# The low half of split weights: a subtraction on VectorE against an accumulating DMA on the negated high half

## The chip, the cores and the metric

The kernel runs on one core of one Trainium2 chip. The metric is the device time of one execution in microseconds (us); three executions of the kernel before took 793.93, 794.14 and 794.63 us, so the median is 794.14 us.

## The reference, cut to what matters

The reference is one layer of a diffusion backbone in float32: 512 latent tokens and 256 context tokens of width 1024 go through one combined input projection into two token mixers (latent attention with 4 heads, and a two-directional gated recurrence, HGRN, with 4 heads), an output projection, and a gated feed-forward network of inner width 2816.

```
h = modulate(rmsnorm(x)), hc = modulate(rmsnorm(ctx))
cq, ckv, kpe, hq, hi, hg, ff, fb = split(h @ w_in)          # same for hc
x = x + gt1 * (concat(attention, hgrn) @ w_out)
h2 = modulate(rmsnorm(x))
x = x + gt2 * ((silu(h2 @ w_gate) * (h2 @ w_up)) @ w_down)
out = rmsnorm(x)
```

Every large product is made to near float32 accuracy out of reduced-precision products. A matrix W is split as W = hi + lo, where hi is W rounded to the format float32r and lo = W - hi, and the other operand likewise; the product is then hi·hi + hi·lo + lo·hi.

## The kernel before, in words

**Blocks of weights.** All weights of the large products stand in a list `units` (lines 103 to 115) of 105 blocks, each 128 partitions by up to 1024 columns of float32 (512 KB): blocks 0 to 24 are the input projection (`wi`), 25 to 28 the attention up-projections (`wqkv`; block 26 has 512 columns), 29 to 36 the output projection (`wo`), 37 to 80 gate and up of the feed-forward network in turn (`wgu`), and 81 to 104 its down projection (`wd`), three blocks for each of eight output tiles: two of 1024 columns and one of 768.

**Making a block.** `make_unit(i)` (lines 119 to 134) loads block i into a tile `wf` by a DMA issued from SyncE's queue (SP), lets ScalarE (ACT) round it into `wh` (line 132, named CAST in the trace) and lets VectorE (DVE) subtract `wh` from `wf` into `wl` (line 133). The tiles `wf`, `wh` and `wl` have three buffers each. `wf` is free for another load when line 133 is done with it; `wh` and `wl` are free when the last matmul that reads them is done. Blocks 33 to 36 have buffers of their own (`rh`, `rl`), and so has block 40 (`xh`, `xl`). `unit(i, ahead)` makes all blocks up to i + ahead before block i is used, so block i+2 is asked for just before the matmuls of block i; since three buffers go round, it takes the buffer of block i-1.

**Using a block.** `mm3` (lines 148 to 152) issues three matmuls: high by high (line 150), a product with one low half (151) and a product with the other (152). In most places the weights are the stationary operand, and then `wl` is first read by the third matmul of a block. In the feed-forward network a block of 1024 columns gives 24 matmuls of 512 columns. For the last of the eight output tiles (line 1053) the tokens are done in two halves of 256, which makes the first pass over its blocks half as long.

**The order on the engines.** The kernel is written with a tile framework. It works out one fixed order of instructions for each engine ahead of time, from the order of the program, priorities and its own model of durations, and each engine then runs its list strictly in order; an instruction that waits for a semaphore holds up what stands behind it on the same engine. The list of the GpSimd engine (POOL) holds a few memsets, four additions `a2` in the recurrence (line 592), and a copy with two memsets for the attention's keys (lines 830 to 832); no DMA is issued from it.

**Neighbours that matter.** `late_mod` (lines 422 to 429) loads 32 further blocks (`wl<-in_wmt_dram` in the trace: the load's name, the tile is one of the three `wf` buffers) and reduces each on VectorE. `gates` (line 467) evaluates two sigmoids on ScalarE after each gate projection. `mla_kpe` (line 709), `make_q`, `make_qr`, `make_v` and `make_k` (lines 762 to 803) lead over to the attention, with high and low halves made by a copy on ScalarE and a subtraction on VectorE. `wout`, `add_sq` and `norm2` (lines 931 to 968) are the output projection, the squares for the second norm, and that norm.

Of the kernel before, what the change touches and what calls it, by code (L numbers as in the profile page):

```python
# [10 lines left out]
F32 = mybir.dt.float32  # L11
# [3 lines left out]
AF = mybir.ActivationFunctionType  # L15
ALU = mybir.AluOpType
# [36 lines left out]
def block_kernel(ctx: ExitStack, tc: tile.TileContext, xT, ctxT, vec, cin, cst, msk, wm, wmt, wi, wqkv, wo, wgu, wd, out):  # L53
    nc = tc.nc
# [7 lines left out]
    def nm(s):  # L62
        uid[0] += 1
        return f"{s}_{uid[0]}"
# [47 lines left out]
    for n in range(KT):  # L112
        for part in range(3):
            w = UNIT if part < 2 else DFF - 2 * UNIT
# [4 lines left out]
    def make_unit(i):  # L119
        kind, src, w = units[i]  # L120
        f = L0.tile([P, UNIT], F32, tag="wf", name=nm("wf"), bufs=3)
        nc.sync.dma_start(f[:, :w], src)
        if kind == "wo" and i >= WO0 + 4:
            hi = stage["pool"].tile([P, UNIT], F32R, tag="rh", name=nm("rh"), bufs=4)
            lo = stage["pool"].tile([P, UNIT], F32R, tag="rl", name=nm("rl"), bufs=4)
        elif i == GU0 + 3:
            hi = N2.tile([P, UNIT], F32R, tag="xh", name=nm("xh"), bufs=1)
            lo = N2.tile([P, UNIT], F32R, tag="xl", name=nm("xl"), bufs=1)
        else:
            hi = L0.tile([P, UNIT], F32R, tag="wh", name=nm("wh"), bufs=3)  # L130
            lo = L0.tile([P, UNIT], F32R, tag="wl", name=nm("wl"), bufs=3)
        nc.scalar.copy(hi[:, :w], f[:, :w])  # L132
        nc.vector.tensor_sub(lo[:, :w], f[:, :w], hi[:, :w].bitcast(F32))  # L133
        made.append((hi, lo))

    WO0 = NW_IN + 4
# [3 lines left out]
    def prefetch(n):  # L140
        while len(made) < min(n, len(units)):
            make_unit(len(made))
# [1020 lines left out]
```

## Time and profile before

One execution was profiled. It took 792.62 us, of which 790.8 us are its span, from the first instruction to the last.

| engine | busy us | share of the span |
|---|---|---|
| TensorE, matmuls (PE) | 768.1 | 97% |
| VectorE (DVE) | 446.9 | 57% |
| ScalarE (ACT) | 311.4 | 39% |
| GpSimd (POOL) | 10.1 | 1% |
| DMA, queue of SyncE | 87.03 MB | 33.0% of 16 engines |

The mean granted clock of TensorE was 0.988. A line such as "L133 DVE TENSOR_TENSOR wl<-wf,wh x100 | 119.6, 1196 | ..." is read thus: line 133 of the kernel ran 100 times on VectorE, writing `wl` from `wf` and `wh`, was busy for 119.6 us in all and 1196 ns each; behind the second bar stands the time for which the engine had been idle just before, and what ended that. Buffer numbers are left out of the names. Matmuls overlap in the pipeline, so that one shown with 0.39 us follows the one before it after 0.23 us.

### The profile page before, as it was taken

What the parts mean: (1) busy time and instruction counts of PE and PEld (TensorE: products, weight loads), DVE (VectorE), ACT (ScalarE), POOL (GpSimd) and SP (SyncE); (2) the same over time, 40 slices, a digit from 0 to 9 for tenths busy, and PEclk for the clock granted to TensorE, in tenths of its full rate; (3) what the DMA queues carried; (4) which work ended last, traced back from release to release, by engine and by line L of the source; (5) the groups of instructions that cost most, each with busy time, mean ns of one, the idle gap of its engine ahead of it and who ended that gap; (6) DMA issues with size and microseconds to landing.
All of it is one profiled execution on the core that took longest, in us unless ns stands there. A gap on an engine that the chain in (4) does not pass through costs nothing.

```text
span 790.8 us, 10832 instructions
## 1 busy us (share of the span) xinstructions
PE 768.1 (97%) x4342; PEld 631.7 (80%) x4342; DVE 446.9 (57%) x820; ACT 311.4 (39%) x569; POOL 10.1 (1%) x18
## 2 busy tenths in 40 slices
PE   8899999999999989999999999999999999999995
PEld 7568878788887768888999888888888888888885
DVE  5576569839778989985566434432333233223324
ACT  6344246434544577664344223222322222212211
POOL 0000000000000100000000000000000000000000
PEclk8899999999999999999999999999999999999997
DMA  9923723311110022345403343423232323332303
GB/s 332 390 76 134 252 80 108 133 57 55 64 55 28 28 80 90 125 165 181 160 2 100 113 160 133 151 89 107 80 107 82 104 78 96 93 100 80 111 3 107
DMA packets 26706, 88.77 MB, mean 112 GB/s; under 512 B 2976, under 2 KB 5280, under 8 KB 26528
## 3 DMA queue, kind: packets, MB, share of 16 engines
q1 hardware_dynamic: 25568, 87.03, 33.0%
q10 hardware_dynamic: 1088, 1.05, 0.4%
q8 instruction: 34, 0.56, 0.3%
q14 instruction: 16, 0.13, 0.1%
HBM read 85.97 MB, written 2.10 MB: 111 GB/s over the span
## 4 chain that ended last, share of the span: by engine, by line
PE 89%; DVE 7%; ACT 2%; issue 1%; DMA 1%; SPq 0%; DVEq 0%; ACTq 0%
PE big L150 18%; PE big L151 17%; PE big L152 17%; PE sm L150 9%; PE sm L151 9%; PE sm L152 9%; PE big L857 2%; PE sm L604 1%; PE sm L876 1%; PE big L858 1%; PE sm L320 1%; DVE U L585 1%; PE sm L598 1%; DVE acl L309 1%; DVE G L506 1%
## 5 line engine op out<-in xcount | busy, mean ns | idle before, releaser
L133 DVE TENSOR_TENSOR wl<-wf,wh 128x1024 fp32r<-128x1024 f32 (+2 forms) x100 | 119.6, 1196 | 186.3 <-ACT wh L132 186.2
L132 ACT CAST wh<-wf 128x1024 fp32r<-128x1024 f32 (+2 forms) x100 | 102.9, 1029 | 280.3 <-PE big L151 167.6
L150 PE MATMUL big<-h2h,wh 128*128 128x512 f32 (+1 forms) x368 | 140.3, 381 | 0.0
L151 PE MATMUL big<-h2l,wh 128*128 128x512 f32 (+1 forms) x368 | 140.0, 381 | 0.0
L152 PE MATMUL big<-h2h,wl 128*128 128x512 f32 (+1 forms) x368 | 140.0, 381 | 0.0
L151 PEld LDWEIGHTS big<-h2l,wh 128*128 128x128 f32 x368 | 69.2, 188 | 14.6
L150 PEld LDWEIGHTS big<-h2h,wh 128*128 128x128 f32 x368 | 69.2, 188 | 14.4
L152 PEld LDWEIGHTS big<-h2h,wl 128*128 128x128 f32 x368 | 69.2, 188 | 14.4
L150 PE MATMUL sm<-ah,wh 128*128 128x512 f32 (+1 forms) x198 | 73.5, 371 | 0.0
L152 PE MATMUL sm<-ah,wl 128*128 128x512 f32 (+1 forms) x198 | 73.4, 371 | 0.0
L151 PE MATMUL sm<-al,wh 128*128 128x512 f32 (+1 forms) x198 | 73.4, 370 | 0.0
L427 DVE SCALAR_TENSOR_TENSOR wl<-wl,cs 128x1024 f32<-128x1024 f32 x32 | 39.0, 1220 | 33.8 <-DMA wl<-in_wmt_dram 33.8
L150 PE MATMUL big<-wh,hh 128*128 128x512 f32 x96 | 40.2, 422 | 3.3 <-ACT hh L340 1.9
L150 PEld LDWEIGHTS sm<-ah,wh 128*128 128x128 f32 x198 | 37.3, 188 | 7.1
L151 PEld LDWEIGHTS sm<-al,wh 128*128 128x128 f32 x198 | 37.3, 188 | 7.1
L152 PEld LDWEIGHTS sm<-ah,wl 128*128 128x128 f32 x198 | 37.3, 188 | 7.1
L150 PE MATMUL big<-hh,wh 128*128 128x512 f32 x104 | 42.8, 412 | 0.0
L151 PE MATMUL big<-hl,wh 128*128 128x512 f32 x104 | 40.9, 394 | 0.0
L152 PE MATMUL big<-hh,wl 128*128 128x512 f32 x104 | 40.8, 392 | 0.0
L151 PE MATMUL big<-wl,hh 128*128 128x512 f32 x96 | 38.8, 406 | 0.0
L152 PE MATMUL big<-wh,hl 128*128 128x512 f32 x96 | 38.4, 402 | 0.0
L506 DVE RECIPROCAL G<-S 128x528 f32<-128x528 f32 x8 | 27.5, 3432 | 0.1
(326 smaller groups left out, 1353.4 us busy)
## 6 DMA issues: line engine op xcount, KB each, us to landing
wf<-in_wgu_dram SPq DMA_DIRECT2D x44, 512.0 KB, 3.4
wl<-in_wmt_dram SPq DMA_DIRECT2D x32, 512.0 KB, 3.5
wf<-in_wi_dram SPq DMA_DIRECT2D x25, 512.0 KB, 3.9
wf<-in_wd_dram SPq DMA_DIRECT2D x16, 512.0 KB, 3.5
wms<-in_wm_dram SPq DMA_DIRECT2D x11, 512.0 KB, 9.6
wf<-in_wo_dram SPq DMA_DIRECT2D x8, 512.0 KB, 3.5
wf<-in_wd_dram SPq DMA_DIRECT2D x8, 384.0 KB, 3.1
wm<-in_wm_dram SPq DMA_DIRECT2D x5, 512.0 KB, 10.2
```

What stands on the lines that cost most here:

```text
L132: nc.scalar.copy(hi[:, :w], f[:, :w])
L133: nc.vector.tensor_sub(lo[:, :w], f[:, :w], hi[:, :w].bitcast(F32))
L150: nc.tensor.matmul(o, lh, rh, start=start, stop=False, skip_group_check=True)
L151: nc.tensor.matmul(o, lh, rl, start=False, stop=False, skip_group_check=True)
L152: nc.tensor.matmul(o, ll, rh, start=False, stop=stop, skip_group_check=True)
L309: nc.vector.tensor_add(acc_, acc_, sq_)
L320: nc.tensor.matmul(ps[32 * g : 32 * g + 32, :256], csil[:, 4 * j + kk, :], f[:, kk * 256 : (kk + 1) * 256], start=(j == 0), stop=(j == 1), ...
L427: nc.vector.scalar_tensor_tensor(f, f, 1.0, sc, op0=ALU.mult, op1=ALU.mult, accum_out=acc)
L506: nc.vector.reciprocal(I, S)
L585: nc.vector.scalar_tensor_tensor(U[:, c1, :], U[:, c0, :], er[:, 1, c0 : c0 + 1], U[:, c1, :], op0=ALU.mult, op1=ALU.add)
L598: nc.tensor.matmul(t, a2[:, j, :], vt[:, j, h * P : (h + 1) * P], start=True, stop=False, skip_group_check=True)
L857: nc.tensor.matmul(ps[:, 0, :], L, R[:, :NL], start=(i == 0), stop=(i == 4), skip_group_check=True)
```

## The change

Blocks 0 to 7 are made as before. From block 8 on, ScalarE writes the negated rounded weight into the low tile (a copy with scale -1), a DMA issued from GpSimd's queue adds the float32 block onto it in SBUF (the destination is viewed as float32, so lo = f - round(f)), and ScalarE rounds the block into the high tile in a second pass. VectorE has no part in these 97 blocks. `wf` is now free when both that DMA and the second pass have read it, and the first matmul that reads the low half waits for the DMA.

```
-        nc.scalar.copy(hi[:, :w], f[:, :w])
-        nc.vector.tensor_sub(lo[:, :w], f[:, :w], hi[:, :w].bitcast(F32))
+        if i < 8:
+            nc.scalar.copy(hi[:, :w], f[:, :w])
+            nc.vector.tensor_sub(lo[:, :w], f[:, :w], hi[:, :w].bitcast(F32))
+        else:
+            nc.scalar.activation(lo[:, :w], f[:, :w], AF.Copy, scale=-1.0)
+            nc.gpsimd.dma_start(lo[:, :w].bitcast(F32), f[:, :w], accum_op=ALU.add)
+            nc.scalar.copy(hi[:, :w], f[:, :w])
```

## The prediction

> **What bounds the kernel now.** I read the page first: who is busy, the chain that ended last, and the two groups that the change touches.
>
> ```profile
> span 790.8 us, 10832 instructions
> ...
> PE 768.1 (97%) x4342; PEld 631.7 (80%) x4342; DVE 446.9 (57%) x820; ACT 311.4 (39%) x569; POOL 10.1 (1%) x18
> ...
> PE 89%; DVE 7%; ACT 2%; issue 1%; DMA 1%; SPq 0%; DVEq 0%; ACTq 0%
> ...
> L133 DVE TENSOR_TENSOR wl<-wf,wh 128x1024 fp32r<-128x1024 f32 (+2 forms) x100 | 119.6, 1196 | 186.3 <-ACT wh L132 186.2
> L132 ACT CAST wh<-wf 128x1024 fp32r<-128x1024 f32 (+2 forms) x100 | 102.9, 1029 | 280.3 <-PE big L151 167.6
> ```
>
> TensorE is busy for 768.1 of 790.8 us and holds 89% of the chain. The subtraction takes VectorE 1196 ns and the rounding takes ScalarE 1029 ns, each 100 times (five more blocks with buffers of their own stand in other groups). Neither is a bound on average, so I look at where TensorE has gaps, by stage (columns: window, its length, then busy time and count for PE, PEld, DVE, ACT, POOL, then clock, DMA share, GB/s).
>
> ```profile
> 230.00:300.00 70.00, 65.38 (x493) 50.89 (x493) 60.21 (x123) 44.60 (x104) 5.05 (x5) 1.00 0.15 49
> 300.00:366.00 66.00, 64.17 (x370) 54.97 (x369) 55.31 (x109) 41.33 (x83) 0.00 (x0) 1.00 0.42 144
> 366.00:420.00 54.00, 54.00 (x394) 51.04 (x393) 36.25 (x76) 24.67 (x46) 0.00 (x0) 1.00 0.27 88
> 420.00:640.00 220.00, 220.00 (x988) 179.29 (x987) 85.39 (x100) 66.51 (x83) 0.00 (x0) 1.00 0.34 113
> 640.00:762.00 122.00, 122.00 (x523) 98.11 (x522) 36.22 (x43) 29.27 (x39) 0.00 (x0) 1.00 0.29 87
> ```
>
> From 366 to 762 us TensorE has no gap: nothing can be won there, only lost, if a low half comes late. The gaps that a lighter VectorE could close lie in 230 to 300 us, the last recurrence head and the passage into attention: 70.00 − 65.38 = 4.62 us. Two of the waits there are on VectorE:
>
> ```profile
> PE big L150 <- DVE krl L720: 1.6, 1, 1.6
> ...
> PE sm L604 <- DVE U L585: 0.6, 1, 0.6
> ```
>
> **What the change moves.** VectorE loses 97 subtractions, 97 × 1.196 = 116 us. ScalarE gains 97 passes; I price one like the rounding of the same shape, 97 × 1.029 = 100 us. GpSimd gains 97 DMA issues, the DMA engines 97 transfers that read two blocks and write one. SP issues what it issued, but a `wf` buffer now comes free only when the transfer has landed.
>
> **How late is the low half?** No row shows an accumulating DMA or a DMA issued from GpSimd. The nearest rows are plain loads and GpSimd's own arithmetic:
>
> ```profile
> wf<-in_wgu_dram SPq DMA_DIRECT2D x44, 512.0 KB, 3.4
> ...
> wf<-in_wd_dram SPq DMA_DIRECT2D x8, 384.0 KB, 3.1
> ...
> x<-in_xT_dram SPq DMA_DIRECT2D x1, 2048.0 KB, 7.8
> ```
>
> ```profile
> 267.18 1.27 POOL L592 TENSOR_TENSOR a<-am,am 128x512 f32<-128x512 f32 x1 [27.58 <-DVE am L559]
> ```
>
> A plain load of 512 KB lands after 3.4 us, four times as much after 7.8 us, so each further 512 KB costs (7.8 − 3.4)/3 = 1.5 us. An accumulation reads twice: 3.4 + 1.5 = 4.9 us. For the issue I take one GpSimd instruction, 1.27 us: L = 6.2 us from the end of the negation to the landing. The lower end is a plain load, 3.4 us; the upper is three in a row (both reads one after the other, behind a weight load in flight), 10.2 us. I take 6.2 because the engines are mostly free (DMA share 0.29 to 0.34 in the feed-forward stages). For 384 KB I take 0.7 us less, 5.5 us.
>
> [...]
>
> **Where L is covered.** In the gate and up stage one block's rounding starts when its buffer is released, and this is its first low use:
>
> ```profile
> 559.12 1.05 ACT L132 CAST wh<-wf 128x1024 fp32r<-128x1024 f32 x1 [2.04 <-PE big L151]
> ...
> 570.78 0.40 PE L152 MATMUL big<-h2h,wl 128*128 128x512 f32 x1
> ```
>
> That is two blocks of matmuls and a little, 11.66 us. The negation has to wait for the last L152 rather than the last L151 (one matmul, 0.2 us later) and takes 1.05 us: L may be 11.66 − 0.2 − 1.05 = 10.4 us. In the down projection two blocks can be 24 + 18 instead of 48 matmuls, 11.2 × 42/48 = 9.8 us, and L may be 9.0 us. With 6.2 both stages cost nothing, and the cover is two blocks of matmuls; beyond 9.0 us the excess would appear in every round of three blocks.
>
> **Term 1, the last head (+1.05 us).** The rounding of a later block stands ahead of the sigmoids, released by the same projection:
>
> ```profile
> 231.76 1.05 ACT L132 CAST wh<-wf 128x1024 fp32r<-128x1024 f32 x1 [3.45 <-PE big L151]
> ...
> 232.71 0.81 ACT L470 ACTIVATE sg<-big 128x768 f32<-128x768 f32 x1
> ...
> 236.09 1.26 DVE L496 TENSOR_TENSOR_SCAN S<-G,reset 128x528 f32<-128x528 f32 x1 [0.51 <-ACT G L493]
> ```
>
> Now two passes stand there. The sigmoids, and behind them the scan for which VectorE sits idle already, come 1.05 us later; that chain ends in the 0.6 us wait of L604, so the whole pass shows. Bounds 0 (the order puts a pass elsewhere) to 1.05.
>
> **Term 2, ACT before attention (+0.9 us).** ScalarE alone, in order:
>
> ```profile
> 282.94 1.04 ACT L132 CAST wh<-wf 128x1024 fp32r<-128x1024 f32 x1
> 285.41 0.28 ACT L610 ACTIVATE osq<-sm 128x128 f32<-128x128 f32 x1 [1.42 <-PE sm L604]
> ...
> 296.06 0.85 ACT L768 CAST knh<-sm 128x512 fp32r<-128x512 f32 x2
> ```
>
> From 285.41 on it runs with almost no gap to the keys at 296.06, for which the first scores wait. Two blocks are made in the 5 us before: 2 × 1.05 = 2.1 us extra, against 1.42 us of idle here; with the negation's later start I put 0.9 us on this run. One VectorE subtraction in the same stretch (1.2 us) goes, which helps only if ScalarE is not late: bounds −1.2 to +1.0.
>
> **Term 3, the krl wait (−0.9 us).**
>
> ```profile
> 269.26 1.21 DVE L133 TENSOR_TENSOR wl<-wf,wh 128x1024 fp32r<-128x1024 f32 x1
> 270.49 0.42 DVE L720 TENSOR_TENSOR krl<-big,krh 64x256 fp32r<-64x256 f32 x1
> ```
>
> This subtraction stands right ahead of the `krl` step that frees TensorE's bank (the 1.6 us wait). Without it the step could start about 1.2 us earlier, but ScalarE's copies from that bank come next; I take 0.9 of it. Bounds −1.2 to 0.
>
> **Term 4, the tail (+0.7 us).** The last output tile is done in halves, so its blocks are needed sooner:
>
> ```profile
> 758.34 1.05 ACT L132 CAST wh<-wf 128x1024 fp32r<-128x1024 f32 x1 [4.57 <-PE sm L151]
> ...
> 762.51 0.84 ACT L132 CAST wh<-wf 128x768 fp32r<-128x768 f32 x1 [3.12 <-PE sm L151]
> ...
> 765.60 0.28 PE L152 MATMUL sm<-ah,wl 128*128 128x256 f32 x1
> ...
> 768.41 0.28 PE L152 MATMUL sm<-ah,wl 128*128 128x256 f32 x1
> ```
>
> Each negation starts about 0.2 us after the cast did (the last L152). Block 103 is negated by 758.5 + 1.05 = 759.55 and lands at 765.75 against a need at 765.60. Block 104: 762.75 + 0.84 + 5.5 = 769.1 against 768.41, 0.7 us late, and this is TensorE's last work: it adds to the end in full. Bounds 0 (L up to 4.8) to 4.5 (L = 10.2).
>
> **Term 5, output projection (+1.0 us).** Here casts wait for loads, and the squares of the norm stand behind them on ScalarE:
>
> ```profile
> 382.61 1.05 ACT L132 CAST xh<-wf 128x1024 fp32r<-128x1024 f32 x1 [2.72 <-DMA wf<-in_wgu_dram]
> ...
> 394.45 0.42 ACT L938 ACTIVATE sqt<-x 128x256 f32<-128x256 f32 x1 [2.40 <-DVE x L951]
> ...
> 397.48 0.26 ACT L190 ACTIVATE rsr<-sm,epst 128x2 f32<-128x2 f32 x1 [1.31 <-PE sm L174]
> ```
>
> Each of the three `wf` buffers is held about 5 us longer (1.05 + 6.2 against 1.03 + 1.2); blocks 38 to 40 are two reuses behind block 32, so their casts move from about 383 to 393 us. If ScalarE's order stays, the last square slips about 3.5 us past 394.87 and TensorE, in order, stands at the sums; if the order adapts, nothing. Bounds 0 to 3.5; I take 1.0, nearer to the adapted order, since the framework orders by its own durations.
>
> GpSimd's other work (four additions, one copy, two memsets) waits behind transfers whose negation waits for TensorE; I cost it at nothing, since TensorE uses those results only several us later. If that cover is gone, the additions delay L598 by up to one issue, 1.3 us.
>
> Sum: 1.05 + 0.9 − 0.9 + 0.7 + 1.0 = +2.75 us: 792.62 + 2.75 = 795.4 us for a profiled execution; the median of the runs lies 1.5 us above the profiled one (794.14), so 796.9 us. A measurement of this kernel can tell about 0.2%, 1.6 us, from no change.
>
> **Rivals.** *Hidden everywhere (0.28):* terms 1, 2 and 5 fall into idle time, leaving the tail less part of term 3: about +0.5 us, 794.6. For it: ScalarE is 39% busy, and 100 us more make 52%. Against it: the two places where ScalarE has no room.
>
> *VectorE was the bound between 230 and 300 us (0.12):* ScalarE's passes fall into its gaps (the 1.42 us), and the removed subtractions come off the chain: −0.9, −1.2 and the 0.6 us of L604: −2.7 us, 791.4. For it: VectorE is busy 60.21 of 70 us there. It decides if the second pass does not precede the sigmoids.
>
> *The low half lands late (0.15):* at L = 10.2 the down projection loses 1.2 us in each of seven rounds, 8 us, the tail 4.5, the output projection 3.5: with terms 1 to 3 about +17 us, 811. It decides from L = 9.0 on. For it: no row shows such a transfer, and GpSimd may be slow to issue. Against it: DMA share near 0.3. [...]
>
> **How the numbers follow.** The forecast has 0.45 (own range 795.8 to 800), the rivals as above. Slower by over 0.2%: 0.45 + 0.15 = 0.60; within: 0.28; faster: 0.12. The range 793 to 806 takes in the hidden case and the start of the late one; it leaves out most of the faster rival and the far half of the late one.
>
> **What would show it.** Right: GpSimd's DMAs landing 5 to 8 us after the negation; no gap on TensorE between 420 and 760 us; a gap near 768 us of up to 1 us before an L152; the scan near 236 us about 1 us later; the krl wait under 1 us. Wrong: waits of TensorE on `wl` in the feed-forward stages (late landing), or a shorter 230 to 300 us stage (VectorE was the bound). A different order of ScalarE around 380 to 400 us settles term 5.

## The result, and the profile after

The changed kernel took 822.68 us (median of 818.55, 819.25, 826.12 and 826.85) against 794.05 us for the kernel before on the same chip: a ratio of 1.036 [1.029, 1.043]. On a second chip it was 820.27 against 792.99 us, 1.036 [1.031, 1.040]. So it is slower, as forecast, but by 28.6 and 27.3 us instead of 2.75, far beyond the range of 793 to 806.

The page of the changed kernel (826.12 us, span 824.2):

```profile
span 824.2 us, 11070 instructions
...
PE 782.5 (95%) x4342; PEld 640.9 (78%) x4342; DVE 339.6 (41%) x723; ACT 396.8 (48%) x666; POOL 94.4 (11%) x115
...
q0 software_dynamic: 13968, 49.55, 33.0%
q1 hardware_dynamic: 25568, 87.03, 31.9%
...
PE 63%; DMA 18%; DVE 8%; ACT 5%; issue 5%; SPq 1%; POOL 0%; DVEq 0%; ACTq 0%; POOLq 0%
...
L138 ACT CAST wh<-wf 128x1024 fp32r<-128x1024 f32 (+2 forms) x92 | 94.3, 1025 | 232.4 <-PE big L156 84.8
...
L137 POOL DMA_DIRECT2D wl<-wf x92 | 79.4, 863 | 544.9 <-ACT wl L136 466.8
...
L136 ACT ACTIVATE wl<-wf 128x1024 fp32r<-128x1024 f32 (+2 forms) x92 | 94.9, 1032 | 26.0 <-DMA wf<-in_wi_dram 15.1
...
wl<-wf POOLq DMA_DIRECT2D x83, 512.0 KB, 5.7
wf<-in_wgu_dram SPq DMA_DIRECT2D x44, 512.0 KB, 4.8
```

VectorE is 107 us lighter and ScalarE 85 us heavier (116 and 100 were worked out). What the forecast did not have stands in two other rows: DMA holds 18% of the chain (1% before), and the new queue q0 takes 33.0% of the sixteen DMA engines, as much as all loads together (q1). By the time of its packets that is 0.330 × 824.2 / 97 = 2.8 us of all sixteen for one accumulation; a load of 512 KB (0.524 MB) takes 0.319 × 824.2 × 0.524 / 87.03 = 1.6 us. A `wgu` load now lands after 4.8 us, before after 3.4.

The windows of time that the prediction showed for the kernel before, with the same columns (the work in them stands 7 to 33 us later, so they do not hold quite the same stages):

```profile
230.00:300.00 70.00, 64.43 (x519) 50.76 (x519) 54.94 (x126) 41.99 (x101) 10.86 (x11) 0.99 0.36 82
300.00:366.00 66.00, 60.94 (x327) 52.07 (x326) 50.42 (x98) 45.29 (x83) 1.72 (x2) 0.90 0.39 114
366.00:420.00 54.00, 49.17 (x276) 42.22 (x275) 17.41 (x36) 27.00 (x42) 7.06 (x9) 0.97 0.80 207
420.00:640.00 220.00, 214.16 (x1044) 178.18 (x1045) 52.90 (x106) 99.33 (x132) 29.52 (x35) 0.98 0.75 185
640.00:762.00 122.00, 122.00 (x523) 98.16 (x523) 12.18 (x20) 50.77 (x64) 19.35 (x23) 1.00 0.84 186
```

TensorE, without a gap from 366 to 762 us before, now has gaps up to 555 us and none after; the DMA share has gone from about 0.3 to 0.75 to 0.84; and the clock (the third column from the end) is below 1.00 in four of five rows. What TensorE waits for (us in total, times, longest):

```profile
PE sm L179 <- DVE sqa L945: 4.5, 1, 4.5
PE big L157 <- DMA wl<-wf: 2.9, 4, 1.3
PE big L862 <- ACT pp L868: 2.8, 1, 2.8
PE big L155 <- DVE qnl L781: 2.7, 1, 2.7
...
PE sm L157 <- DMA wl<-wf: 2.3, 1, 2.3
PE sm L881 <- DVE oml L892: 2.2, 1, 2.2
```

Only two rows are waits on the low half itself, 5.2 us in all. The longest is the wait for the squares of the norm, term 5. Its cause can be read in two views of the same stretch, first ScalarE's list in order of time (in brackets its idle time and what ended it):

```profile
398.11 1.06 ACT L136 ACTIVATE rl<-wf 128x1024 fp32r<-128x1024 f32 x1 [7.14 <-DMA wf<-in_wo_dram]
...
410.46 1.06 ACT L136 ACTIVATE wl<-wf 128x1024 fp32r<-128x1024 f32 x1 [5.95 <-DMA wf<-in_wgu_dram]
411.42 0.71 ACT L943 ACTIVATE sqt<-x 128x256 f32<-128x256 f32 x2
...
414.20 1.06 ACT L136 ACTIVATE wl<-wf 128x1024 fp32r<-128x1024 f32 x1 [1.13 <-DMA wf<-in_wgu_dram]
...
418.48 1.06 ACT L136 ACTIVATE xl<-wf 128x1024 fp32r<-128x1024 f32 x1 [1.96 <-DMA wf<-in_wgu_dram]
```

and the chain of waits:

```profile
385.31 4.57 DMA rl<-wf
389.87 0.02 SPq L122
389.89 0.04 issue
389.94 8.15 DMA wf<-in_wo_dram
...
399.46 4.54 DMA rl<-wf
404.00 0.02 SPq L122
404.02 0.04 issue
404.06 6.29 DMA wf<-in_wgu_dram
```

An accumulation lands at 389.87, and only then is its `wf` free and SP starts the next load, which takes 8.15 us beside the other transfers; once round, 404.00 and 6.29 us. ScalarE stands 5.95 us in front of the negation for that block (block 38), and the squares, which need none of it, stand behind it; 1.13 and 1.96 us more follow in front of the negations for blocks 39 and 40. TensorE is idle from 418.20 to 422.66. I call this a **late load at the head of a line**.

To locate the loss I take, block by block, how much later TensorE first uses it than in the trace before. Its growth by stretch, in us:

| kernel (one profile each) | to block 23 | to 29 | to 33 | to 41 | to 61 | to the end | sum |
|---|---|---|---|---|---|---|---|
| changed | 4.1 | 10.7 | 4.2 | 7.8 | 4.0 | 0.2 | 31.1 |
| changed, second chip (816.12 us) | 1.3 | 7.3 | 3.7 | 7.7 | 1.1 | 0.2 | 21.4 |

Block 2 starts the count: in the first 46 us, before any changed block is used, profiles differ by up to 7 us by chance (most stand 2 to 3 us later than that of before, three 1 us earlier or so, one 5.5 us later), and that is left out here. Blocks 23, 29, 33, 41 and 61 are first used at 234, 355, 382, 430 and 542 us of the trace before.

**The clock.** In the row of 300 to 366 us above the clock column reads 0.90: TensorE is busy for 60.94 us there, part of them at half speed. The trace's clock records give full speed in the kernel before from 24 to 782 us; in the changed kernel they have six stretches of 3.41 or 6.83 us at half clock, behind the gaps of 2.2 to 4.5 us at 148, 295, 310, 340, 395 and 418 us, 27.3 us in all. Half of that, up to 13.7 us, is lost without any wait that a view shows. On the second chip it was 13.7 us at half clock.

### The profile page after: what moved, and what is told of

It reads as the page before. It is cut to its first block, busy times and chain, and to the rows that moved or that the text cites. A ratio compares the mean times of both kernels' runs of the same rounds, so it can differ in the third digit from the quotient of the medians.

```text
span 824.2 us, 11070 instructions
## 1 busy us (share of the span) xinstructions
PE 782.5 (95%) x4342; PEld 640.9 (78%) x4342; DVE 339.6 (41%) x723; ACT 396.8 (48%) x666; POOL 94.4 (11%) x115
## 3 DMA queue, kind: packets, MB, share of 16 engines
q1 hardware_dynamic: 25568, 87.03, 31.9%
q10 hardware_dynamic: 1088, 1.05, 0.4%
## 4 chain that ended last, share of the span: by engine, by line
PE 63%; DMA 18%; DVE 8%; ACT 5%; issue 5%; SPq 1%; POOL 0%; DVEq 0%; ACTq 0%; POOLq 0%
PE big L155 12%; PE big L156 12%; PE big L157 12%; PE sm L155 6%; PE sm L156 6%; PE sm L157 6%; DMA wf<-in_wgu_dram 4%; DMA wl<-wf 4%; DMA wf<-in_wi_dram 4%; DMA wl<-in_wmt_dram 2%; DMA wf<-in_wo_dram 2%; PE big L862 1%; DVE wl L432 1%; PE sm L609 1%; DMA rl<-wf 1%
## 5 line engine op out<-in xcount | busy, mean ns | idle before, releaser
L138 ACT CAST wh<-wf 128x1024 fp32r<-128x1024 f32 (+2 forms) x92 | 94.3, 1025 | 232.4 <-PE big L156 84.8
L137 POOL DMA_DIRECT2D wl<-wf x92 | 79.4, 863 | 544.9 <-ACT wl L136 466.8
L136 ACT ACTIVATE wl<-wf 128x1024 fp32r<-128x1024 f32 (+2 forms) x92 | 94.9, 1032 | 26.0 <-DMA wf<-in_wi_dram 15.1
L1006 DVE TENSOR_TENSOR sgl<-sgl,big 128x512 f32<-128x512 f32 x22 | 15.1, 687 | 161.3 <-ACT sgl L1005 161.3
L155 PEld LDWEIGHTS big<-h2h,wh 128*128 128x128 f32 x368 | 69.2, 188 | 14.1
L1037 DVE SCALAR_TENSOR_TENSOR x<-sm,mod,x 128x512 f32<-128x512 f32 (+1 forms) x9 | 6.2, 691 | 97.6 <-PE sm L157 97.6
```

The source lines that it names most:

```text
L136: nc.scalar.activation(lo[:, :w], f[:, :w], AF.Copy, scale=-1.0)
L137: nc.gpsimd.dma_start(lo[:, :w].bitcast(F32), f[:, :w], accum_op=ALU.add)
L155: nc.tensor.matmul(o, lh, rh, start=start, stop=False, skip_group_check=True)
L1006: nc.vector.tensor_mul(sg, sg, ps[:, 1, :])
L1037: nc.vector.scalar_tensor_tensor(x1[:, n, a : a + w], ps[:, :w], mod[:, 3, n : n + 1], x1[:, n, a : a + w], op0=ALU.mult, op1=ALU.add)
```

## The experiments

Each is compared with the kernel before on its own chip (median, ratio and 95% interval); stretches are those of the table above, in us. First the changed kernel once more:

> The changed kernel once more, on the chip of these runs: 818 to 828 us, with the same places of loss (150, 260 to 300, 311, 340, 395, 418 and 500 to 555 us) if they belong to the kernel; places that are missing here are chance.

Five of those places came again; the gap near 150 us was 1.2 instead of 2.3 us with no half clock behind it, and 500 to 555 us lost 1.1 us instead of 4.0. So those two vary from run to run, which fits the spread of 816 to 827 us.

The theory that I began with: `wf` is held until the accumulation has landed, so loads come late, and a late load at the head of a line does the rest. Rival A: ScalarE's second pass. Rival B: the traffic of the transfers.

**A VectorE addition in place of the transfer** (label e1_dve_add)

```
-            nc.gpsimd.dma_start(lo[:, :w].bitcast(F32), f[:, :w], accum_op=ALU.add)
+            nc.vector.tensor_add(lo[:, :w], f[:, :w], lo[:, :w].bitcast(F32))
```

> The negation and the rounding stay on ScalarE, but the sum that makes the low half is a VectorE addition on the tile instead of a transfer; it computes the same. Theory (the transfer holds a wf buffer for about 6 us, the next load starts that much later, and ScalarE's negation, waiting for that load, blocks what stands behind it): the buffer comes free about 1.2 us after the passes, as before the change, so nearly all of the 28 us goes: 793 to 798 us, no gap of TensorE of 2 us or more after 30 us, no half clock there. Rival A (ScalarE's second pass is what costs): 810 us or more, with the gaps at 148, 296, 311, 340 and 419 us still there.

798.56 against 794.62 us, 1.0052 [1.0030, 1.0074]. Stretches: 0.7, 4.4, 0, 0, 0, 0. Rival A falls for everything from block 29 on; its stages are full again:

```profile
366.00:420.00 54.00, 54.00 (x365) 49.71 (x364) 31.99 (x65) 30.64 (x50) 0.00 (x0) 1.00 0.31 109
420.00:640.00 220.00, 220.00 (x1019) 180.69 (x1018) 86.37 (x109) 101.85 (x124) 0.00 (x0) 1.00 0.32 110
```

But the second pass is not free: 4.4 us between blocks 23 and 29, more than I expected of it (the median lies just above the range of 793 to 798), and there a gap of 3.58 us with half clock behind it.

**The accumulation reads the block from HBM again** (label e2_hbm_cast), so that `wf` is free after ScalarE's passes

```
-            nc.gpsimd.dma_start(lo[:, :w].bitcast(F32), f[:, :w], accum_op=ALU.add)
+            nc.gpsimd.dma_start(lo[:, :w], src, accum_op=ALU.add)
```

> The accumulating transfer reads the weight block from HBM a second time instead of from its wf buffer, so the buffer is free when ScalarE's two passes are done; transfers and their landing stay, and the low half is as late as before or later; it computes the same up to the type in which the sum is rounded. Theory (held buffer, late load): loads start early again, most of the loss goes: 796 to 804 us, and at most the places stay where TensorE waits for wl itself (block 32, blocks 47 to 59: up to 8 us). Rival B (the late landing itself, or the traffic of the transfers, costs): 815 us or more.

816.64 us, 1.026 [1.021, 1.032]. My expectation failed. Stretches: 0, 10.0, 6.5, 0, 1.7, 1.9. Between blocks 33 and 41, where the squares stood behind late loads, the loss is gone (0 instead of 7.8 and 7.7); the other stretches tell less, since before block 23 and behind block 41 the two profiles of the changed kernel differ by about 3 us themselves. But these transfers, which read HBM and write the float32r tile, take longer (median 7.6 us to landing, 5.7 in the changed kernel), and at block 32 TensorE waits 4.8 us for the low half itself:

```profile
383.26 11.49 DMA wl<-in_wo_dram
394.76 0.04 issue
394.80 0.79 PE sm L157
```

So this form has a cost that isn't the held buffer: transfers that take longer, 11.49 us at block 32. How much of it the changed kernel's own transfers have, this run can't tell.

**The negation on GpSimd** (label e5_pool_neg)

```
-            nc.scalar.activation(lo[:, :w], f[:, :w], AF.Copy, scale=-1.0)
+            nc.gpsimd.tensor_scalar(lo[:, :w], f[:, :w], -1.0, None, op0=ALU.mult)
```

> The negation moves from ScalarE to GpSimd; the accumulating transfer stays; ScalarE has a single pass for each block again; it computes the same. Theory (held buffer): the buffer is held as long or longer (GpSimd's pass is no faster than ScalarE's), loads stay late; ScalarE's rounding waits for them in the negation's place: 812 to 830 us. Rival A (ScalarE's second pass costs): 794 to 802 us.

835.99 us, 1.054 [1.051, 1.057]. Rival A falls again: ScalarE has its single pass (311.4 us busy, as before) and the loss is larger. The negation takes 2.7 us on GpSimd (1.03 on ScalarE in the changed kernel), so the low half and the release of `wf` are that much later.

**Only from block 61 on** (label e3_from61)

```
-        if i < 8:
+        if i < 61:
```

> The changed form only from block 61 on (the end of the modulation loads), so 44 of the 97 blocks; it computes the same. Theory: there every block has slack for the landing and no other user of the wf buffers; no loss before 530 us, nothing behind it: 793 to 797 us. Rival B (the transfers' traffic or the low half's landing costs for every block alike): 44/97 of 28 us, 804 to 810 us.

794.19 us, 0.9997 [0.9975, 1.0019]. Stretches: 0 everywhere, 0.1 at the end. 44 of 97 transfers cost nothing, although the DMA engines are as busy as in the changed kernel:

```profile
550.00:640.00 90.00, 90.00 (x388) 72.50 (x387) 11.04 (x16) 40.47 (x49) 13.76 (x16) 1.00 0.83 184
```

**Traffic without a hold, and with one** (labels e7_traffic and e8_hold): the kernel before, and beside it an accumulation into a buffer in HBM that nobody reads

```
+        if i >= 8:   # e7_traffic: hi[:, :w].bitcast(F32) as source; e8_hold: f[:, :w]
+            nc.gpsimd.dma_start(scr[i][:, :w], SOURCE, accum_op=ALU.add)
```

> The kernel before (rounding on ScalarE, subtraction on VectorE), and beside it GpSimd issues for every block from the ninth on an accumulating transfer of the rounded block (wh) into memory that nobody reads: the traffic of the change, but it holds no wf buffer and nobody waits for it; it computes the same. Rival B (traffic): loads take longer and the loss comes back, 805 us or more. Theory (held wf buffer): wh is held some us longer than a matmul needs it at most; 794 to 799 us.

> The same with the transfer reading the wf buffer instead of wh, so that the next load into that buffer waits for the end of the transfer, about 5 us later than before; no second pass on ScalarE, no low half that comes late; it computes the same. Theory (held wf buffer): loss at the places where loads were late after the change (near 150 us, 410 to 440 us, blocks 47 to 59), 8 to 20 us: 803 to 815 us, the difference to the run with wh as source is 8 us or more. Rival B: no more than 3 us apart from the run with wh as source.

812.88 us, 1.022 [1.018, 1.027], and 808.12 us, 1.017 [1.013, 1.021]. For the first my theory said 794 to 799: it fell as the only cause. The second lies in the range that I had set, but it was to be 8 us or more above the first and is 4.8 us below it: neither branch of that expectation came true. Stretches with `wh` as source: 1.4, 3.3, 0, 8.8, 6.6, 0.1; with `wf`: 7.1, 0.6, 0, 2.5, 0, 0. Traffic makes loads late with no `wf` held (`wh` is, but no engine's wait in this trace ended with such a transfer). It is not quite the traffic of the change: it goes to HBM, and its queue takes 36.0% of the engines, 3.0 us for each transfer instead of 2.8:

```profile
scr_dram<-wh POOLq DMA_DIRECT2D x83, 512.0 KB, 5.6
wf<-in_wgu_dram SPq DMA_DIRECT2D x44, 512.0 KB, 5.4
```

and the consequence is the picture of the changed kernel, the squares (L940 here) behind a rounding that waits for its load, after a load of 9.56 us in the chain:

```profile
401.04 1.04 ACT L132 CAST xh<-wf 128x1024 fp32r<-128x1024 f32 x1 [5.96 <-DMA wf<-in_wgu_dram]
401.99 1.04 ACT L132 CAST wh<-wf 128x1024 fp32r<-128x1024 f32 x1
402.93 0.72 ACT L940 ACTIVATE sqt<-x 128x256 f32<-128x256 f32 x2
```

With `wf` as source a load cannot start while the transfer that reads its buffer runs, and from block 29 on less is lost than with `wh`. So hold and traffic do not simply add up.

**Short and long stalls of TensorE** (labels g1_short and g2_long), to price the clock: the kernel before, with a chain of VectorE copies before each of the output tiles 1 to 7 of the down projection

```
+        if n and a == 0:
+            c = N2.tile([P, 256], F32, tag="sqt", name=nm("gap"), bufs=4)
+            nc.vector.tensor_copy(c[:, :W], x1[:, n - 1, :W])
+            for _ in range(K):              # g1_short: W = 32, K = 0; g2_long: W = 256, K = 8
+                nc.vector.tensor_copy(c[:, :W], c[:, :W])
+            nc.vector.tensor_copy(ps[:, :W], c[:, :W])
```

> The kernel before, with seven short stalls of TensorE in the down projection: at the start of output tiles 1 to 7 its accumulator waits for two small VectorE copies behind the step before; it computes the same. About 1.1 us each by the durations of such copies: 7 x 1.1 = 8 us, so 800 to 804 us. Theory of the clock (a gap from about 2 us on is followed by 3.4 us or twice that at half clock, a shorter one is not): no half clock behind them, the loss is the sum of the gaps. Rival: every gap costs clock, 805 us or more.

> The same with chains of ten VectorE copies, seven gaps of about 3 to 4 us; it computes the same. Theory of the clock: behind each gap 3.4 to 6.8 us at half clock, which costs 1.7 to 3.4 us besides: the loss is 1.4 to 2 times the sum of the gaps, 825 to 845 us. Rival (the half clock seen in the trace after has another cause): the loss is the sum of the gaps alone, 815 to 822 us, no half clock.

822.85 us, 1.035 [1.031, 1.040], and 850.68 us, 1.071 [1.067, 1.076]. The "short" stalls were not short: seven of 18.6 / 7 = 2.66 us (the wait row), and a window before, in and behind one of them reads:

```profile
PE sm L150 <- DVE sm L1032: 18.6, 7, 2.8
```

```profile
685.00:692.00 7.00, 7.00 (x31) 5.42 (x29) 1.23 (x1) 1.10 (x2) 0.00 (x0) 1.00 0.35 97
692.00:695.00 3.00, 0.21 (x2) 0.10 (x1) 2.57 (x6) 1.50 (x3) 0.00 (x0) 1.00 0.36 133
695.00:702.00 7.00, 7.00 (x24) 5.58 (x25) 0.00 (x0) 0.00 (x0) 0.00 (x0) 0.76 0.15 52
```

Behind the gap 7 us hold 24 matmuls instead of 31, at 0.76 of the clock. Six of the seven gaps are followed by 3.41 us at half clock. The kernel loses 29.4 us at the end of this trace, of which 18.6 are waits; the other 10.8 are close to half of 6 × 3.41 = 20.5. In the long case the gaps were 5.1 to 5.8 us instead of 3 to 4; all seven (39.3 us of waits) are followed by 6.83 us at half clock, and 57.4 us are lost. So these gaps cost 1.6 and 1.5 times their length on average, and the half clock belongs to gaps, not to this change. A fixed length from which on a gap costs clock, as the expectation had it, does not hold: one of the gaps of 2.79 us here and one of 2.84 us on the second chip (at 307 us) had no half clock behind them, and one of 1.84 us there (at 388 us) had.

**Blocks 29 to 60 alone** (label x1_29to60) **and every second block** (label x2_every2nd)

```
-        if i < 8:
+        if i < 29 or i > 60:     # x1_29to60;  x2_every2nd: if i < 8 or i % 2:
```

> The changed form for blocks 29 to 60 alone (output projection, and the gate and up blocks beside which modulation rows are loaded), 32 of the 97 blocks; it computes the same. Theory (loads, accumulations and modulation loads together come near the capacity of the DMA engines there; with the held buffers that makes loads late): about what the trace after lost between the uses of blocks 29 and 60, some 12 to 16 us: 806 to 812 us. Rival (those losses only follow from the delays before them, or each of the 97 blocks costs alike): 32/97 of 28 us or less, 803 us or less.

> The changed form for every second block only, from the ninth on; it computes the same. Theory (the DMA engines' capacity decides from block 29 on): with half the transfers their share falls to about 0.7 in the gate and up stage, no loss at blocks 41 to 60, at most 4 us in the output projection, half or less of the rest before: 797 to 805 us. Rival (each changed block costs alike): half of 28 us, 808 us.

814.14 us, 1.028 [1.025, 1.030], 2 us above the expected range; stretches -0.2, 5.0, 3.7, 8.2, 2.0, 0.1. And 804.66 us, 1.014 [1.012, 1.017]; 0, 3.0, 0.5, 5.8, 0, 0. A third of the blocks makes 21 of the 27 us that the whole change costs on this chip. One reading is the rate of the DMA engines: in part of the output projection TensorE takes 2.8 us for a block (blocks 33 to 36), while a load and an accumulation take 1.6 + 2.8 = 4.4 us of all DMA engines, and their share is 0.98, 0.97 and 0.93 in the three windows of 10 us from 390 us of the changed kernel. Between blocks 41 and 55 it is 4.4 plus half a modulation load, 5.2 of the 5.6 us that TensorE takes for a block, and behind them 4.4 of 5.6 (estimates from these prices; the measured share is 0.88 from 460 to 555 us, and 0.83 from 560 to 640). With half the transfers that stage is at 0.65 and loses nothing:

```profile
460.00:550.00 90.00, 90.00 (x387) 72.53 (x386) 27.07 (x37) 33.81 (x41) 6.88 (x8) 1.00 0.65 181
```

In the output projection (to 33 and to 41) 6.3 us are left of the 11.9 that blocks 29 to 60 alone lose there. The losses go by stage, not by the number of transfers.

**Blocks 24 to 31 subtracted by GpSimd** (label x5_pool_sub), the version that was to win

```
-        nc.vector.tensor_sub(lo[:, :w], f[:, :w], hi[:, :w].bitcast(F32))
+        eng = nc.gpsimd if 24 <= i < 32 else nc.vector
+        eng.tensor_sub(lo[:, :w], f[:, :w], hi[:, :w].bitcast(F32))
```

> A version meant to win: the kernel before, with the subtraction for blocks 24 to 31 on GpSimd instead of VectorE; no second pass on ScalarE, no transfer; it computes the same. If VectorE's subtraction was what stood ahead of the krl step and the scan between 230 and 300 us, TensorE gains up to 2.7 us: 791 to 794 us against 794. If GpSimd's slower pass makes the low half late for TensorE or holds the wf buffer too long: 795 to 800 us.

809.61 us, 1.021 [1.018, 1.024]: both branches of the expectation were wrong. All 16.2 us are lost between blocks 23 and 29. One part shows: a VectorE step that took 0.68 us before (line 788 there) takes 2.40 us beside a GpSimd pass, and ends 0.55 us after it (VectorE's and GpSimd's lists):

```profile
291.48 2.40 DVE L789 SCALAR_TENSOR_TENSOR m<-m,cs 128x512 f32<-128x512 f32 x1
```

```profile
290.98 2.35 POOL L134 TENSOR_TENSOR wl<-wf,wh 128x1024 fp32r<-128x1024 f32 x1 [4.37 <-ACT wh L132]
```

That stretch has no version here that beats the kernel before.

**Blocks 8 to 23, blocks 24 to 28, and these with an addition** (labels y1_8to23, y2_24to28, y3_24to28_add): the condition set to those blocks, in the last with the VectorE addition shown above

> The changed form for blocks 8 to 23 alone; it computes the same, and TensorE's work stays in the order of the kernel before. Theory (a held wf buffer makes a modulation load or weight load late near 130 to 155 us): 1.5 to 5 us, 795 to 799 us. If the loss near 150 us was chance: 793 to 795 us.

> The changed form for blocks 24 to 28 alone; it computes the same, but TensorE's work near 240 to 300 us stands in the other order that the changed kernel has too. The trace after lost about 5 us between the uses of blocks 23 and 28: 797 to 801 us if these blocks cause it; 793 to 795 us if it followed from earlier delays.

> Blocks 24 to 28 alone with negation and rounding on ScalarE and a VectorE addition, no transfer; it computes the same. If ScalarE's second pass and the order are the cause: as much as with the transfer, within 2 us. If the transfer is the cause: 793 to 795 us.

796.08 us, 1.0030 [1.0007, 1.0053]; 801.29 us, 1.010 [1.005, 1.016]; 798.97 us, 1.0066 [1.0040, 1.0092]. Sums in their profiles: 3.1, 7.1 and 4.4 us. With 18.9 for blocks 29 to 60 and 0.1 from 61 on the parts give 3.1 + 7.1 + 18.9 + 0.1 = 29.2 us, between the two profiles of the whole change and near its 28 us. Of the 7.1 us of blocks 24 to 28, 4.4 come without any transfer, from the second pass and from the other order in which the framework then puts the work (block 24 is begun about 3 us earlier in both runs; block 27 0.4 us later with the addition and 5.6 with the transfer). The other 2.7 us come with the transfer. By the medians the two runs differ by 2.3 us, so neither branch of the last expectation is quite met. How much is the pass and how much the order isn't separated.

**A hold without a transfer** (labels y5_hold_only, two passes; y6_hold_half, one)

```
+        if 29 <= i <= 60:
+            for _ in range(2):
+                nc.gpsimd.tensor_scalar(f[:, :w], f[:, :w], 1.0, None, op0=ALU.mult)
```

> The kernel before, and behind the subtraction of blocks 29 to 60 two GpSimd passes over wf in place (times one), which hold the buffer about 5.4 us longer by the 2.7 us of such a pass; no transfer, no second pass on ScalarE; it computes the same. Theory of the held buffer: most of the 20 us that blocks 29 to 60 lose, 804 to 814 us. Theory of the full DMA engines: 793 to 798 us.

> As the run with two GpSimd passes over wf, with one: blocks 29 to 60 hold their buffer about 2.9 us longer than before, GpSimd is at most half busy in the feed-forward stage; no transfer; it computes the same. Theory of the held buffer: some of the loss is back, in the output projection above all, where a block takes TensorE 2.8 us and three buffers turn round: 797 to 805 us, none in the feed-forward stage. If only GpSimd's own rate made the loss with two passes: 793 to 796 us.

830.55 us, 1.046 [1.042, 1.050], and 797.01 us, 1.0029 [1.0010, 1.0048]. Stretches with two passes: 0, 8.6, 0, 19.0, 7.7, 0.1; with one: -0.2, 2.1, 0, 2.4, 0, 0.1. Loads take 3.4 and 3.2 us (before 3.4), so a hold without any transfer can lose as much and more. But the first of these two runs overshoots, because GpSimd itself was full and held the buffers longer than the 5.8 us of two passes:

```profile
L136 POOL TENSOR_SCALAR wf<-wf 128x1024 f32<-128x1024 f32 x64 | 183.8, 2882 | 124.9 <-DVE rl L133 50.3 <-DVE wl L133 33.0 <-ACT qs L796 21.6
```

```profile
380.00:425.00 45.00, 32.59 (x186) 29.40 (x184) 19.87 (x26) 11.91 (x20) 44.51 (x16) 0.86 0.24 82
```

VectorE is a little slower beside these passes too (its twelve sums of squares between 280 and 440 us took 561 ns each, 422 before), so even this is not a hold and nothing else. A hold of 2.8 us costs 4.4 us where the change loses 18.9, and the change holds about 4.8 us longer than before (1.05 + 6 against 1.03 + 1.2). **What stays open:** which share of the 19 us from block 29 to 60 is the hold and which the full DMA engines. Each costs time without the other (18.7 us by the medians with traffic alone, 4.4 us with one pass's hold), and in the run that took the hold away the transfers were longer (7.6 against 5.7 us). A fourth `wf` buffer, which would part them, was not tried.

## Why the prediction was wrong, step by step

The step that failed is the price of the transfer. The sum charged ScalarE's second pass (terms 1 and 2) and the landing of the low half in the tail (term 4), and it moved loads by the held buffer in term 5 alone, at +1.0 us. It put at nothing what the transfer takes of the DMA engines, the late loads in the other stages, and the clock behind new gaps. The run without the transfer (the VectorE addition) loses nothing from block 29 on, where the changed kernel lost 16.2 and 12.7 us in its two profiles.

**Right: the landing time.** L was put at 6.2 us; negation to landing was 3.8 to 9.4 us, mostly 4.8 to 7.5. The bounds 3.4 to 10.2 hold. The median from issue to landing was 5.7 us.

**Right: blocks from 61 on, and the tail.** "With 6.2 both stages cost nothing" holds from block 61 (0.1 us in the run from 61 on). Term 4 was put at +0.7 us and measured 0.2: the last two low halves landed 4.8 and 4.3 us after their negation, which is the case "0 (L up to 4.8)" of its bounds.

**Right: term 1.** The last head was put at +1.05 us. With blocks 24 to 28 alone changed the use of block 23 ends 1.0 us later. In that run the negation stands between the sigmoids and the gates' second step, and the scan follows (ScalarE's list, then VectorE's):

```profile
233.85 1.09 ACT L136 ACTIVATE wl<-wf 128x1024 fp32r<-128x1024 f32 x1
...
235.27 0.65 ACT L497 ACTIVATE G<-sg,lb,oml 128x264 f32<-128x264 f32 x1
```

```profile
236.45 1.26 DVE L501 TENSOR_TENSOR_SCAN S<-G,reset 128x528 f32<-128x528 f32 x1
```

**Mis-sized: terms 2 and 3, ScalarE before the attention.** They were +0.9 and -0.9 us. The krl wait of term 3 is gone from the list of waits, but a wait for `qnl` of 2.7 us stands there instead. The list of before had that wait, and one more on VectorE, beside the two that the prediction picked from it:

```profile
PE sm L620 <- DVE ow L614: 1.2, 1, 1.2
...
PE big L150 <- DVE qnl L776: 1.0, 2, 0.7
```

With the addition in place of the transfer this stretch loses about 3 us beyond term 1, with the transfer 6, part of it half clock. The place was right; that the framework would put the work in another order, and the clock, were not in the sum.

**Wrong: "I take 6.2 because the engines are mostly free (DMA share 0.29 to 0.34 in the feed-forward stages)".** The share was used for the latency of one transfer. What a transfer takes of the engines was never worked out: 2.8 us each, which lifts the share to 0.8 and more, and near 1 in the output projection. With it loads get slower (3.4 to 4.8 us), and the sum let every load take what it took before. The run with traffic and no `wf` held loses 18.7 us by the medians.

**Wrong: term 5, the step that failed most.** It was +1.0 us, with bounds 0 to 3.5. The mechanism stood there word for word ("the last square slips ... and TensorE, in order, stands at the sums"), and so did the held buffer; but the whole stretch from block 29 to 41 lost 12.0 us (11.4 on the second chip). About 4.0 of it is the wait for the low half of block 32 (2.3 us) and the half clock behind it (half of 3.41); about 7.9 is the wait for the squares and the half clock behind that (half of 6.83). The slip of the squares itself was thus 4.5 us (4.7 on the second chip), four times the 1.0 and above the bound of 3.5.

The bound was too low because the reuses were: two of about 5 us were to move the pass for block 40 by 10 us. It moved from 382.61 to 418.48 us, and only 17.4 of these 35.9 us were lost before block 29, so 18.5 remain. The loads issued at 389.9, 404.1, 409.1 and 413.1 us each started within 0.1 us of the landing of an accumulation, and took 8.2, 6.3, 5.0 and 5.4 us instead of 3.4. One buffer was loaded at 389.94, 404.06 and 417.24 us, so a round of three blocks took 14.1 and 13.2 us. The nine loads for blocks 35 to 43 went out in 35.6 us, in the trace before in 18.0. By the prediction's own figures a round is 3.4 + 1.05 + 6.2 = 10.7 us, so nine loads would take some 28 us (an estimate: eight steps of a third of a round). By this estimate a hold alone slows them already, and the slower transfers do the rest; no run shows the two shares.

I chose 1.0 because the framework might adapt its order. It did, but not far enough: before, the third pair of squares stood behind the passes for blocks 37 and 38 and the fourth behind those for 40 and 39; now they stand ahead of these, but the fourth is still behind the negation for block 38, and the next two squares behind those for 39 and 40.

**Wrong: nothing was charged to the attention and to blocks 41 to 60.** Modulation loads share the `wf` buffers, so a held buffer also makes them late, and VectorE's reduction stands at the head of its line: an accumulation lands at 336.60 us, the modulation load into its buffer runs from 336.65 to 339.93, the reduction follows, and `oml` behind it is written from 341.45 us on, for which TensorE waits 2.2 us. With blocks 29 to 60 alone changed, 5.0 us are lost before block 29 is used. 4.0 and 1.1 us in the two profiles of the changed kernel were lost at blocks 41 to 60, where I had said that nothing is.

**Missing: the clock.** No term allowed for it; up to 13.7 of the 31.1 us.

The rival "the low half lands late" had the sum nearest to the result (811), but by the wrong road: "it decides from L = 9.0 on" in the down projection, where nothing was lost, and only 5.2 us of waits were on the low half.

## What to carry to other kernels

A new transfer has two prices: its latency, and the time that it takes of all DMA engines; work out the second for each stage against the time that the stage leaves per block, not against the mean share. When a buffer of a rotation is read longer, follow the next load into it and ask what stands behind the first instruction that waits for that load, on its in-order engine; go round the rotation as often as the stage does. Compare the round of the rotation (load, passes, landing) over its number of buffers with the time per block. And count the half clock behind new gaps on TensorE: in the two runs with made gaps, those of 2.66 us on average cost 1.6 times their length and those of 5.1 to 5.8 us 1.5 times.

## What the runs showed of the hardware

**Half clock came behind windows in which TensorE was much idle.** The half-clock stretches of all profiles begin and end, the last one's end aside, on a grid of 3.413 us that keeps its phase through a run; counted from the first instruction, the grid lies differently from run to run. In the trace of the changed kernel the first of them starts at 15.74 us and the last at 817.87, 235 times 3.413 us later. I laid that grid over 19 profiles (from 60 us on, windows at full clock) and took TensorE's idle share in each from the matmuls of the trace:

| idle share of a window | windows | followed by half clock |
|---|---|---|
| under 0.2 | 3842 | 0 |
| 0.2 to 0.5 | 145 | 12 |
| 0.5 to 0.6 | 18 | 13 |
| over 0.6 | 41 | 41 |

So in these profiles a gap counted by how it fell on the grid: of the six gaps of 2.5 to 2.8 us in the run with short stalls one went free; it was split between two windows (idle 0.32 and 0.50). A window did not have to be idle throughout for half clock to follow: about half was enough in some cases, over 0.6 in all 41.

**An accumulation from one tile into another took the DMA engines 1.8 times as long as a load of the same size** (in the changed kernel 2.8 against 1.6 us by the time of the packets), and the third of three in a row (block 32) landed 9.3 us after its negation.

**A VectorE step took three times as long beside GpSimd.** The step of 0.68 us that reads two tiles (`m` and `cs`) runs twice in the trace before, with that time in both. In the run with GpSimd's subtraction it took 2.06 and 2.40 us, and in both it ended 0.55 us after the GpSimd pass beside it (2.36 and 2.35 us long). No run shows what held it up.
